# Five groups of small products per mixer unit in place of fourteen

## The chip, the cores and the metric

The kernel runs on one core of a Trainium2 chip. A core has engines that run side by side, each with its own in-order queue: TensorE (PE, with weight loads listed apart as PEld), VectorE (DVE), ScalarE (ACT), GpSimd (POOL) and SyncE (SP, which here only issues DMAs). Products are written by PE into PSUM, which DVE and ACT read. The metric is the device time in microseconds of one execution; the time before is the median of three runs.

## The reference

One layer of a streaming encoder for 1024 frames of a new stream and 32 frames of a running one:

```
h, st = mixer(rms_norm(x, g_mix_pre), ...)      # three head groups, one input and one output projection
x = x + rms_norm(h, g_mix_post)
h, buf = conv_ffn(rms_norm(x, g_ffn_pre), ...)  # up, causal conv, gelu gate, down
x = x + rms_norm(h, g_ffn_post)
```

The mixer has 6 GLA heads (keys of 32), 5 HGRN2 heads and 5 mLSTM heads (keys of 64). GLA and HGRN2 are gated linear scans in chunks of 64 positions:

```
b      = cumsum(log_a)                                     # per chunk and key channel
scores = einsum('bihd,bjhd,bijhd->bijh', q, k, exp(b_i - b_j))   # j <= i
o      = einsum('bijh,bjhv->bihv', scores, v) + einsum('bihk,bhkv->bihv', q * exp(b), s)
s_new  = exp(b_last) * s + einsum('bjhk,bjhv->bhkv', k * exp(b_last - b), v)
```

mLSTM is alike, with one scalar decay per head and a memory `C` with a normaliser column. Head norms and gates follow, then `cat @ w_out`.

## The kernel before, in words

All large products split each fp32 operand into a high and a low part and take three matmuls (`mm3`, lines 101 to 103). Tokens come in three groups: 0 to 383, 384 to 767, and 768 to 1023 with the 32 sample frames. For each group `inproj` (from line 357) computes the input projection on PE: the feature tiles `pf`, convolutions, decays, then the token-major blocks `pv` of values and gates. In the last group `vg_across` computes these blocks feature-major and turns them back with transposes (`back`, line 448): one of the three units behind the first half of the next block, the other two behind its second half, each in a PSUM bank of its own from the pool `psb`, whose tag `big` has three banks.

The recurrent part is the generator `mixer(u, g, ci0)` (line 722), one call per unit of 128 tokens (units 0 to 7) or of the 32 sample frames (unit 8). A unit has two chunks of 64. The exact pairwise decays are built by levels: for c = 32, 16, 8, 4, 2, 1 the positions are split into blocks of 2c, and the second half of a block scores against its first half with decays relative to the block's middle. For one level:

- DVE and ACT make `x` (difference and exponentials), then `Ld` (keys times decay) and `Qz` (queries times decay, lines 847 and 851). `Ld` and `Qz` have two buffers that alternate by level; `x` has three.
- PE makes 16 products of 64 rows and 64 columns into `sc` (one buffer of two banks), 32 matmul records in the profile.
- DVE copies the level's part into the score matrix `P` with a mask (`put`, line 810; the copy is line 815); for c = 32 ACT copies it.

Then come the diagonal `sd`; the state products `up`, in the half banks that `small` hands out in turn (one bank, named `mi` in the profile); the outputs `og` and `oh` (`P` times v, and `qz` times the state `S`); `finish` (norm and gate); the mLSTM scores `sm` with the weights `w`; the transposes of its keys; the memory products `um`; and `oi` and `om`. `sm`, `og`, `oh`, `om`, `oi` share two PSUM banks (tag `o`). Nearly all small products go through the helper `first` (line 718, the matmul itself shows as line 720), which raises their priority by `AHEAD` = 100. [...]

The order of instructions on each engine is made by a scheduler: it simulates the program in time, and takes of the instructions that are ready the one of highest priority, which is by place in the program, with the raised ones ahead. `tc.issue_after(x)` puts what its block issues on x's engine behind x. The mixer yields after each part, and `merge` advances the mixers of the group before by so many steps (`NMIX` = 17 per unit) while a group's `inproj` (`NIN` steps), or the output projection, goes forward. The mixers of the last group (units 8, 6, 7) run beside the output projection of units 0 to 5 and 8; that of 6 and 7 follows. Then comes the feed-forward part (from about 700 us), which the change doesn't touch.

Of the kernel before, what the change touches and what calls it, by code (L numbers as in the profile page):

```python
# [19 lines left out]
DEC = 32  # L20
# [71 lines left out]
def body(ctx: ExitStack, tc: tile.TileContext, a: dict):  # L92
# [264 lines left out]
    def inproj(g, xh, xl, normed, scaled=None):  # L357
# [88 lines left out]
        def vg_across(blks):  # L446

            def back(blk, fs, part):
                for (u, off, n) in units_of(g)[part]:
                    ps = psb.tile([128, 256], F32, tag="big", name=f"pb{u}_{blk}")  # L450
                    for e in range(2):
                        pe.transpose(ps[:n, 128 * e:128 * e + 128], fs[e][:, off:off + n], ident)
                    vg_store(blk, u, off, n, ps)

            before = None
            for blk in blks:
                ws = vg_weights(blk)
                fs = p1.tile([128, 2, T], F32, tag="x", name=f"vf{blk}", bufs=3)
                fs = [fs[:, 0], fs[:, 1]]
                for e in range(2):  # L460
                    ps = psb.tile([128, T], F32, tag="big", name=f"pv{g}_{blk}_{e}")
                    for k in range(8):
                        mm3(ps, [w[:, 128 * e:128 * e + 128] for w in ws[k]], (xh[:, k, :], xl[:, k, :]), k == 0, k == 7)
                    act.copy(fs[e], ps)
# [5 lines left out]
            for e in range(2):  # L470
                back(*before, slice(e, 1 + 2 * e))
# [78 lines left out]
        def rows():  # L550
# [52 lines left out]
            dcs = mx.tile([128, 3, 8], F32, tag="dcs", name=f"dcs{g}", bufs=2)  # L603
            cl = mx.tile([128, 3, 128], F32, tag="cols", name=f"cols{g}", bufs=2)
            if g:
                with tc.high_priority(offset=AHEAD):
                    act.copy(dcs[:, :, :ci], dcp[:, :, :ci])
            for i0, i1 in ((0, 3),) if g == 0 else ((0, 2), (2, 3)):
                if g:
                    yield  # L610
                pt = own[:, :3] if g == 0 else small(i1 - i0, 128)
                for i in range(i0, i1):
                    u, off, n = us[i]
                    pe.transpose(pt[:n, i - i0, :], st[:, off:off + n], ident)
                n = us[i0][2]
                with tc.high_priority(offset=AHEAD):
                    act.copy(cl[:n, i0:i1], pt[:n, :i1 - i0])
                for i in range(i0, i1):
                    cols_of[us[i][0]] = cl[:, i]
            if g == 0:  # L620
# [97 lines left out]
    def first(fn, *args, **kw):  # L718
        with tc.high_priority(offset=AHEAD):
            fn(*args, **kw)  # L720

    def mixer(u, g, ci0):
# [71 lines left out]
        for f0 in (0, 2):  # L794
            kps = small(2, 128)
            for f in (f0, f0 + 1):
                first(pe.transpose, kps[:n, f - f0, :], khf[:, f * n:f * n + n], ident)
            for ch, (o, m) in enumerate(chunks):
                with tc.high_priority(offset=AHEAD):
                    act.copy(kt2[o:o + m, ch, 128 * f0:128 * f0 + 256], kps[o:o + m].rearrange("p f n -> p (f n)"))  # L800
# [23 lines left out]
        li = 0  # L824
        for c in levels:
# [20 lines left out]
            li += 1  # L846
# [7 lines left out]
            sc = psm.tile([128, 1024], F32, tag="sc", name=f"sc{u}_{c}", bufs=1)  # L854
            sc = sc[:, :11 * SCW].rearrange("p (h s) -> p h s", s=SCW)
            for j in range(4):
                for (o, m) in chunks:
                    for hf in range(2):
                        f, q0, q1, p0 = HALVES[hf][j]
                        r = slice(64 * hf, 64 * hf + 64)  # L860
                        mm = c if c == levels[0] else m
                        first(pe.matmul, sc[o:o + mm, p0:p0 + q1 - q0, :m // 2], L[r, f, o:o + mm],
                              Q[r, q0:q1, o // 2:(o + m) // 2], start=True, stop=True)
            if c == levels[0]:
                for (o, m) in chunks:
                    act.copy(P[o:o + c, :, c:2 * c], sc[o:o + c, :, :c])
            else:
                put(c, sc[:n, :, :cl // 2])
            if c == 2:
# [3 lines left out]
                sd = small(11)  # L873
                for f in range(4):
                    first(pe.matmul, sd[:n], z[:, f * n:f * n + n], of_head[:, f, :], start=f == 0, stop=f == 3)
# [6 lines left out]
        Ss = []  # L882
        for ch, (o, m) in enumerate(chunks):
            S = state["S", u == 8]
            Ss.append(S)
            up = small(4, 64)
            for (f, r0, dk, vc) in HEADS:
                first(pe.matmul, up[r0:r0 + dk, f, :], kt2[:n, ch, 128 * f + r0:128 * f + r0 + dk], v[:n, vc:vc + 64],
                          start=True, stop=True)
            Sn = mx.tile([128, 4, 64], F32, tag="S", name=f"S{u}_{ch}", bufs=3)  # L890
            dve.tensor_tensor(Sn, S, dec[:, :, ch:ch + 1].broadcast_to([128, 4, 64]), op=ALU.mult)
            si = dve.tensor_tensor(Sn, Sn, up, op=ALU.add)
            state["S", u == 8] = Sn
        yield

        for (h0, h1, ot) in ((0, 6, og), (6, 11, oh)):
            for h in range(h0, h1):
                f, r0, dk, vc = HEADS[h]
                for ch, (o, m) in enumerate(chunks):
                    first(pe.matmul, ot[o:o + m, OUT[h], :], P[o:o + m, PLANE[h], :m], v[o:o + m, vc:vc + 64],  # L900
                          start=h == h0, stop=False, skip_group_check=True)
        for (h0, h1, ot) in ((0, 6, og), (6, 11, oh)):
            for h in range(h0, h1):
                f, r0, dk, vc = HEADS[h]
                for ch, (o, m) in enumerate(chunks):
                    first(pe.matmul, ot[o:o + m, OUT[h], :], qz[:, h, o:o + m], Ss[ch][:, f, :],
                          start=False, stop=h == h1 - 1, skip_group_check=True)
# [4 lines left out]

        cat = mx.tile([128, 1024], F32, tag="cat", name=f"cat{u}", bufs=1) if u != 7 else ring[0]("cat7")
        ss = mx.tile([128, 16], F32, tag="hss", name=f"hss{u}", bufs=2)
        rs = mx.tile([128, 16], F32, tag="hrs", name=f"hrs{u}", bufs=2)
# [18 lines left out]
        mq, mk = m6[:, 0:3, :], m6[:, 3:6, :]  # L934
        act.copy(mqz[0:64, 0:5:2, :n], mq[0:64, :, :])
        act.copy(mqz[64:128, 1:4:2, :n], mq[64:128, 0:2, :])
        sm = psm.tile([128, 5, 64], F32, tag="o", name=f"sm{u}", bufs=2)
        for f in range(3):
            rows, hs = (128, slice(2 * f, 2 * f + 2)) if f < 2 else (64, slice(4, 5))
            for (o, m) in chunks:  # L940
                first(pe.matmul, sm[o:o + m, hs, :m], mk[:rows, f, o:o + m], mqz[:rows, hs, o:o + m], start=True, stop=True)
        w = mx.tile([128, 320], F32, tag="w", name=f"w{u}", bufs=1)
        w3 = w[:n, :5 * cl].rearrange("p (h n) -> p h n", n=cl)
        dve.tensor_tensor(w3, ab3[:n], cols[:n, 0:5].unsqueeze(2).broadcast_to([n, 5, cl]), op=ALU.add)
        dve.tensor_tensor(w3, w3, caus[:n, :cl].unsqueeze(1).broadcast_to([n, 5, cl]), op=ALU.min)
        act.activation(w3, w3, AF.Exp)
        dve.tensor_tensor(w3, w3, sm[:n, :, :cl], op=ALU.mult)
        yield
        for (h0, h1) in ((0, 4), (4, 5)):
            kp = small(4, 64)  # L950
            if h0 == 0:
                for f in range(2):
                    first(pe.transpose, kp[:n, 2 * f:2 * f + 2, :].rearrange("p h d -> p (h d)"), mk[:, f, :], ident)
            else:
                first(pe.transpose, kp[:n, 0, :], mk[:64, 2, :], ident[:64, :64])
            for ch, (o, m) in enumerate(chunks):
                kwi[0] = dve.tensor_tensor(kw2[o:o + m, ch, h0:h1], kp[o:o + m, :h1 - h0],
                                           cols[o:o + m, 96 + h0:96 + h1].unsqueeze(2).broadcast_to([m, h1 - h0, 64]), op=ALU.mult)
        Cs = []
        for ch, (o, m) in enumerate(chunks):  # L960
            C = state["C", u == 8]
# [956 lines left out]
```

## Time and profile before

| | |
|---|---|
| median of 3 runs | 1377.89 us (1376.87 to 1379.1) |
| profiled execution | 1378.88 us, span of the profile 1377.1 us |
| granted PE clock | 0.989 |
| PE busy | 1326.5 us (96%) |
| DVE busy | 1029.4 us (75%) |
| ACT busy | 705.0 us (51%) |
| POOL busy | 313.1 us (23%) |
| mean DMA rate | 196 GB/s |

An engine's busy time is the time in which at least one of its instructions runs. Matmuls overlap in a pipeline, so what one costs is read from the distance between starts, not from its own duration. A row of the timeline has the start and length in us, engine, line, operation, the output and inputs by name, the weights' rows*columns, the form and a count; idle time before it stands in brackets with what ended it. The mixers' products lie between about 150 and 650 us.

### The profile page before, as it was taken

Reading aid. Unit: us, or ns where it says so; the run is one execution under the profiler, and the core shown is the slowest. Engines: PE = TensorE matmul, PEld = TensorE weight load, DVE = VectorE, ACT = ScalarE, POOL = GpSimd, SP = SyncE. Lnnn points to the kernel's source line nnn. Section 1 sums busy time; section 2 is a strip of 40 time slices with the busy share of each in tenths; the row PEclk is TensorE's granted clock in tenths of the full one; section 3 lists DMA queues with packets and bytes.
Section 4 is the critical chain, followed back from the end, with each engine's and each line's share of the span. In section 5 each row is a group of like instructions: output and inputs, shape, how many; then the busy total and the mean of one; then the engine's idle time right before and its main releaser. Section 6 shows DMA issues by size and latency. Waiting matters only on the chain.

```text
span 1377.1 us, 29219 instructions
## 1 busy us (share of the span) xinstructions
PE 1326.5 (96%) x11472; PEld 1198.8 (87%) x11472; DVE 1029.4 (75%) x1916; ACT 705.0 (51%) x1369; POOL 313.1 (23%) x529
## 2 busy tenths in 40 slices
PE   6999999999999898999989999999999999999997
PEld 5999889898889786867879999999999997678885
DVE  4786458768587669685989888888888876399566
ACT  4555447445475547342665555555455545454552
POOL 5532411226012154222211112111121110010005
PEclk9999999999999999999999999999999999999998
DMA  9699778876789936543423565655374239744435
GB/s 342 203 318 363 262 243 284 260 262 207 262 261 316 336 96 198 176 130 88 168 66 116 163 177 136 150 141 156 107 184 129 87 113 394 274 152 133 147 110 123
DMA packets 125825, 269.72 MB, mean 196 GB/s; under 512 B 24007, under 2 KB 59367, under 8 KB 125607
## 3 DMA queue, kind: packets, MB, share of 16 engines
q1 hardware_dynamic: 111959, 245.43, 52.9%
q0 software_dynamic: 8928, 18.09, 7.1%
q10 hardware_dynamic: 4800, 4.33, 0.9%
q8 instruction: 90, 1.47, 0.4%
q14 instruction: 48, 0.39, 0.1%
HBM read 206.72 MB, written 86.18 MB: 213 GB/s over the span
## 4 chain that ended last, share of the span: by engine, by line
PE 75%; DVE 10%; DMA 6%; ACT 5%; issue 2%; POOL 1%; SPq 1%; DVEq 0%; ACTq 0%; POOLq 0%
PE pux L101 4%; PE pux L102 4%; PE pux L103 4%; PE pv L101 4%; PE pv L103 4%; PE pv L102 4%; PE puw L102 3%; PE puw L103 3%; PE puw L101 3%; PE q L101 3%; PE q L102 3%; PE q L103 3%; PE x L101 2%; PE x L102 2%; PE x L103 2%; PE zp L101 2%
## 5 line engine op out<-in xcount | busy, mean ns | idle before, releaser
L1341 DVE SCALAR_TENSOR_TENSOR y<-uu,fconv_sb,y 128x1060 f32<-128x1060 f32 x88 | 116.2, 1321 | 36.7 <-ACT y L1339 35.8
L1277 ACT COPY c<-pux 128x272 f32<-128x272 f32 (+1 forms) x132 | 49.3, 376 | 50.1 <-PE pux L103 46.5
L101 PE MATMUL pv<-wt_0h,xh 128*128 128x256 f32 (+2 forms) x195 | 57.7, 296 | 5.4 <-ACT xh L321 4.8
L1339 ACT ACTIVATE y<-uu,fconv_sb 128x1060 f32<-128x1060 f32 x44 | 56.1, 1274 | 12.1 <-POOL uu L1335 10.8
L101 PE MATMUL zp<-woh,ch 128*128 128x512 f32 (+1 forms) x144 | 59.4, 414 | 2.4 <-DVE z L1156 1.2
L1338 POOL COPY fhalo<-uu 128x2 f32<-128x2 f32 x44 | 17.1, 388 | 184.2 <-DVE uu L1282 184.2
L102 PE MATMUL zp<-wol,ch 128*128 128x512 f32 (+1 forms) x144 | 57.9, 402 | 0.0
L103 PE MATMUL zp<-woh,cl 128*128 128x512 f32 (+1 forms) x144 | 57.8, 402 | 0.0
L103 PE MATMUL pv<-wt_1h,xl 128*128 128x256 f32 (+2 forms) x195 | 57.1, 293 | 0.0
L103 PE MATMUL pv<-wt_0h,xl 128*128 128x256 f32 (+2 forms) x195 | 56.7, 291 | 0.4 <-DVE xl L322 0.4
L101 PE MATMUL pv<-wt_1h,xh 128*128 128x256 f32 (+2 forms) x195 | 56.9, 292 | 0.0
L102 PE MATMUL pv<-wt_1l,xh 128*128 128x256 f32 (+2 forms) x195 | 56.8, 291 | 0.0
L102 PE MATMUL pv<-wt_0l,xh 128*128 128x256 f32 (+2 forms) x195 | 56.2, 288 | 0.1
L1517 POOL TENSOR_TENSOR gss<-gss 128x1 f32<-128x1 f32 (+1 forms) x9 | 8.1, 899 | 186.8 <-ACT gjk L1510 186.8
L220 POOL TENSOR_SCALAR hrs<-hss 128x5 f32<-128x5 f32 (+3 forms) x27 | 9.6, 356 | 161.2 <-DVE hss L922 159.8
L101 PEld LDWEIGHTS pv<-wt_0h,xh 128*128 128x128 f32 (+1 forms) x195 | 36.8, 189 | 7.4 <-ACT xh L321 5.7
L431 POOL TENSOR_TENSOR vg<-vth,gh 128x256 f32<-128x256 f32 (+1 forms) x36 | 29.2, 812 | 61.6 <-DMA vm<-v_d 22.0
L815 DVE COPY_PREDICATED P<-masks_sb,sc 128x352 f32<-128x352 int32 (+1 forms) x44 | 29.8, 677 | 11.8 <-PE sc L720 11.5
L851 DVE TENSOR_TENSOR Qz<-x,qe 128x128 f32<-128x128 f32 (+1 forms) x106 | 29.8, 298 | 11.7 <-PE sc L720 11.0
L103 PEld LDWEIGHTS pv<-wt_0h,xl 128*128 128x128 f32 (+1 forms) x195 | 37.1, 190 | 1.2 <-DVE xl L322 0.9
L101 PEld LDWEIGHTS pv<-wt_1h,xh 128*128 128x128 f32 (+1 forms) x195 | 37.6, 193 | 0.4 <-issue 0.2
L103 PEld LDWEIGHTS pv<-wt_1h,xl 128*128 128x128 f32 (+1 forms) x195 | 37.4, 192 | 0.6 <-issue 0.2
(1718 smaller groups left out, 5384.3 us busy)
## 6 DMA issues: line engine op xcount, KB each, us to landing
wrP<-in_w_dn SPq DMA_DIRECT2D x27, 512.0 KB, 3.4
h_d<-y SPq DMA_DIRECT2D x22, 530.0 KB, 2.8
ht<-h_d SPq DMA_DIRECT2D x22, 530.0 KB, 8.8
wt_0r<-in_w_tok SPq DMA_DIRECT2D x21, 512.0 KB, 5.2
wt_1r<-in_w_tok SPq DMA_DIRECT2D x21, 512.0 KB, 6.8
ws_d<-in_w_dn POOLq DMA_DIRECT2D x20, 512.0 KB, 8.7
wrP<-ws_d SPq DMA_DIRECT2D x20, 512.0 KB, 4.2
wt_0l<-lt_d SPq DMA_DIRECT2D x14, 512.0 KB, 4.1
```

What stands on the lines that cost most here:

```text
L101: pe.matmul(ps, lh[0], rh[0], start=first, stop=False, **kw)
L102: pe.matmul(ps, lh[0], rh[1], start=False, stop=False, **kw)
L103: return pe.matmul(ps, lh[1], rh[0], start=False, stop=last, **kw)
L220: pool.tensor_scalar(out, ss, 1.0 / width, eps, op0=ALU.mult, op1=ALU.add)
L431: pool.tensor_tensor(o[:n], th[:n], gh[:n, c0:c0 + 256], op=ALU.mult)
L815: dve.copy_predicated(dst, mk.broadcast_to([n, 11, *mk.shape[2:]]), src)
L851: dve.tensor_tensor(Qp[:, 2 * i, :, :n // 2].rearrange("p e (m c) -> p e m c", c=c), second(x4[:, f:f + 1], c).broadcast_to([128, 2, n // ...
L1277: kept[name] = act.copy(t, ps)
L1338: behind["POOL"] = pool.tensor_copy(fhalo[:, j, :], u[:, NCOL - 2:NCOL])
L1339: act.activation(y, u, AF.Identity, scale=fconv[:, j, 2:3], bias=fconv[:, j, 3:4])
L1341: dve.scalar_tensor_tensor(y, uu[i][:, s:s + NCOL], fconv[:, j, s:s + 1], y, op0=ALU.mult, op1=ALU.add)
L1517: pool.tensor_tensor(ss[:n, 0:1], ss[:n, 2:3], ss[:n, 3:4], op=ALU.add)
```

## The change

A unit's small products are collected into five groups:

1. the scores of the levels 32 and 16, then the transposes of the keys `khf`;
2. the scores of 8 and 4, then the mLSTM scores `sm` and the transposes of its keys;
3. the scores of 2 and 1, then the diagonal `sd` (now in the free columns of the `sc` tile) and the state products of both chunks;
4. the outputs `og` and `oh`, then the memory products `um` of both chunks;
5. `oi` (last chunk first) and `om`.

Two levels share one `sc` tile, side by side. In each group the product whose operands are computed last is issued first (`lead`), and the rest is put behind it with `issue_after`. The level's products start with the features whose `Qz` is written last. DVE and ACT work is the same but is written at other places: the `mqz` copies and the weights `w` come ahead of the second group instead of behind `finish`. The priority of the small products is 400 (`SOON`) instead of 100. Unit 8 has the levels 16 to 1, so its last group of scores has one level.

Beside this, `back` makes the transposes of all three units at once behind the second half of a block, two units in one bank and the third in another; the row statistics of groups 1 and 2 are transposed in one tile of their own in `psb` instead of in half banks of `small`; and `NMIX` is 11, since a unit has 9 steps instead of 15.

```diff
-            def back(blk, fs, part):
-                for (u, off, n) in units_of(g)[part]:
-                    ps = psb.tile([128, 256], F32, tag="big", name=f"pb{u}_{blk}")
+            def back(blk, fs):
+                us = units_of(g)
+                whole = psb.tile([128, 2, 256], F32, tag="big", name=f"pb{us[0][0]}_{blk}")
+                rest = psb.tile([128, 256], F32, tag="big", name=f"pb8_{blk}")
+                pss = [whole[:, 0], whole[:, 1], rest]
+                for (u, off, n), ps in zip(us, pss):
                     for e in range(2):
                         pe.transpose(ps[:n, 128 * e:128 * e + 128], fs[e][:, off:off + n], ident)
+                for (u, off, n), ps in zip(us, pss):
                     vg_store(blk, u, off, n, ps)
...
-                    if before:
-                        back(*before, slice(e, 1 + 2 * e))
+                    if before and e:
+                        back(*before)
...
-            own = psm.tile([128, 4, 128], F32, tag="o", name="rows0", bufs=2) if g == 0 else None
-            dcp = small(3, 8) if g else own[:, 3, :24].rearrange("p (a b) -> p a b", b=8)
+            own = (psb if g else psm).tile([128, 4, 128], F32, tag="big" if g else "o", name=f"rows{g}", bufs=3 if g else 2)
+            dcp = own[:, 3, :24].rearrange("p (a b) -> p a b", b=8)
...
-    def first(fn, *args, **kw):
-        with tc.high_priority(offset=AHEAD):
+    SOON = 400
+
+    def soon(fn, *args, **kw):
+        with tc.high_priority(offset=SOON):
             fn(*args, **kw)
...
+        def scores(sc, c, L, Q, at, lead=None):
+            ins = None
+            with tc.issue_after(lead.ins) if lead else ExitStack():
+                for j in (3, 0, 1, 2):
+                    for (o, m) in chunks:
+                        for hf in range(2):
+                            f, q0, q1, p0 = HALVES[hf][j]
+                            r = slice(64 * hf, 64 * hf + 64)
+                            mm = c if c == levels[0] else m
+                            with tc.high_priority(offset=SOON):
+                                x = pe.matmul(sc[o:o + mm, p0:p0 + q1 - q0, at:at + m // 2], L[r, f, o:o + mm],
+                                              Q[r, q0:q1, o // 2:(o + m) // 2], start=True, stop=True)
+                            ins = ins or x
+            return ins
...
+        for l0 in range(0, len(levels), 2):
+            pair = [operands(c, i) for i, c in enumerate(levels[l0:l0 + 2])]
+            last_pair = pair[-1][0] == levels[-1]
...
+            lead = scores(sc, *pair[-1], (len(pair) - 1) * (cl // 2))
+            if len(pair) == 2:
+                scores(sc, *pair[0], 0, lead)
+            sd = sct[:, 11 * SCW:11 * SCW + 11]
+            with tc.issue_after(lead.ins):
+                if l0 == 0:
+                    keys()
+                elif l0 == 2:
+                    memory_scores()
+                if last_pair:
+                    for f in range(4):
+                        soon(pe.matmul, sd[:n], z[:, f * n:f * n + n], of_head[:, f, :], start=f == 0, stop=f == 3)
+                    si = states()
...
+        lead = None
         for (h0, h1, ot) in ((0, 6, og), (6, 11, oh)):
             for h in range(h0, h1):
                 f, r0, dk, vc = HEADS[h]
                 for ch, (o, m) in enumerate(chunks):
...
+        with tc.issue_after(lead.ins):
+            for (h0, h1, ot) in ((0, 6, og), (6, 11, oh)):
...
+            memories()
...
+        lead = None
+        for ch, (o, m) in reversed(list(enumerate(chunks))):
+            for h in range(5):
+                with tc.high_priority(offset=SOON), tc.issue_after(lead.ins) if lead else ExitStack():
+                    x = pe.matmul(oi[o:o + m, h, :], mqz[:, h, o:o + m], Cs[ch][:, h // 2, :], start=True, stop=True)
+                lead = lead or x
+        with tc.issue_after(lead.ins):
+            for h in range(5):
+                for ch, (o, m) in enumerate(chunks):
+                    soon(pe.matmul, om[o:o + m, h, :], w[o:o + m, h * cl:h * cl + m], vmt[o:o + m, h, :], start=True, stop=True)
...
-    NMIX, NIN = 17, 12 + 2 + 24
+    NMIX, NIN = 11, 12 + 2 + 24
```

The functions `keys`, `memory_scores`, `states` and `memories` hold the products and copies that the loop body had before, in the same form: first the products of both chunks, then the additions on DVE that read them.

More of the change, by code (lines that the diff above doesn't have):

```diff
@@ L469, in vg_across @@
                 yield
-            for e in range(2):
-                back(*before, slice(e, 1 + 2 * e))
+            back(*before)
         tgs = pf.tile([128, 3, 26], F32, tag="tgs", name=f"tgs{g}")
@@ L822, in mixer, with operands @@
                     act.activation(qe[:, i, e, :n], q4[:, f, :], AF.Copy, scale=parity[:, i, e:e + 1])
-        li = 0
-        for c in levels:
+        def operands(c, li):
             x = mx.tile([128, 512], F32, tag="x", name=f"x{u}_{c}", bufs=NX)
@@ L864, in mixer @@
[L864 to L869, printed above, removed]
+            return c, L, Q
+        def scores(sc, c, L, Q, at, lead=None):
[12 more added lines that the diff above has]
+            return ins
@@ new lines, in mixer, with keys @@
+        mq, mk = m6[:, 0:3, :], m6[:, 3:6, :]
+        cat = mx.tile([128, 1024], F32, tag="cat", name=f"cat{u}", bufs=1) if u != 7 else ring[0]("cat7")
+        ss = mx.tile([128, 16], F32, tag="hss", name=f"hss{u}", bufs=2)
+        rs = mx.tile([128, 16], F32, tag="hrs", name=f"hrs{u}", bufs=2)
+        def keys():
+            for f0 in (0, 2):
+                kps = small(2, 128)
+                for f in (f0, f0 + 1):
+                    soon(pe.transpose, kps[:n, f - f0, :], khf[:, f * n:f * n + n], ident)
+                for ch, (o, m) in enumerate(chunks):
+                    with tc.high_priority(offset=AHEAD):
+                        act.copy(kt2[o:o + m, ch, 128 * f0:128 * f0 + 256], kps[o:o + m].rearrange("p f n -> p (f n)"))
@@ L932, in mixer @@
         yield
[L934 to L958, printed above, removed]
```

173 lines of the change are left out of this document (90 added, 83 removed).

## The prediction

> **What bounds the kernel now.** I read the page's busy times first, then the windows that cut the span into stages, then TensorE's (PE's) timeline in the stage that the change touches, then what PE and VectorE (DVE) wait for there.
>
> ```profile
> PE 1326.5 (96%) x11472; PEld 1198.8 (87%) x11472; DVE 1029.4 (75%) x1916; ACT 705.0 (51%) x1369; POOL 313.1 (23%) x529
> ```
> ```profile
> PE 75%; DVE 10%; DMA 6%; ACT 5%; issue 2%; POOL 1%; SPq 1%; DVEq 0%; ACTq 0%; POOLq 0%
> ```
> ```profile
> 150.00:226.00 76.00, 73.99 (x758) 65.80 (x757) 47.52 (x111) 42.79 (x82) 10.80 (x15) 0.98 0.75 244
> 226.00:345.00 119.00, 116.87 (x1523) 108.53 (x1522) 90.99 (x211) 62.99 (x132) 41.01 (x59) 1.00 0.77 255
> 345.00:510.00 165.00, 159.46 (x2012) 143.76 (x2011) 114.99 (x308) 88.29 (x209) 38.72 (x62) 0.98 0.78 261
> 510.00:660.00 150.00, 142.77 (x1457) 109.70 (x1457) 115.71 (x243) 66.08 (x147) 45.20 (x70) 0.98 0.48 148
> ```
> ```profile
> 400.00:450.00 50.00, 47.16 (x608) 43.25 (x604) 41.49 (x108) 30.10 (x70) 9.51 (x20) 0.97 0.94 307
> 510.00:560.00 50.00, 45.26 (x412) 35.47 (x411) 45.08 (x100) 29.34 (x62) 21.53 (x27) 0.97 0.51 163
> ```
>
> The columns behind the length are busy microseconds of PE, weight loads, DVE, ScalarE (ACT) and GpSimd, then PE's clock, the DMA share and GB/s. The mixers lie in 150 to 660 us. PE is busy 493.1 of those 510 us, so 16.9 us are idle, and over the whole span 75% of the chain that ended last (the row that begins with PE 75%) is PE's. Two stretches are different: at 400 to 450 the DMA engines are at 0.94, and at 510 to 560 DVE is busy 45.08 us of 50, as much as PE. What is saved on PE there is not all saved in time. Behind 700 us nothing changes.
>
> How much of PE's time is the mixers' small products? The same windows restricted to their one helper line (720) end in this row:
>
> ```profile
> sum 510.00, PE 141.14 PEld 112.42; mean PE 35.28 PEld 28.11
> ```
>
> That is 141 of 510 us. The small products do not stand in one block per unit. On the timeline PE leaves the large 128*128 matmuls, does some products with 64- or 32-wide tiles, and returns. I call that a visit. There are 99 visits of the mixers, of which these are the beginning of the first and the end of the last:
>
> ```profile
> 153.64 0.55 PE L720 MATMUL sc<-Qz,Ld 64*32 64x64 f32 x32
> ...
> 647.90 0.80 PE L720 MATMUL om<-vm,w 64*64 64x65 f32 x20
> ```
>
> **What a visit costs.** Columns: start, us, line, tile, rows*columns, count.
>
> ```profile
> 238.14 0.34 PE L102 MATMUL pf<-xl,wf_12h 128*128 128x384 f32 x1
> 238.41 0.69 PE L720 MATMUL sc<-Qz,Ld 64*64 64x64 f32 x32
> 239.02 0.45 PE L103 MATMUL pf<-xh,wf_12l 128*128 128x384 f32 x1
> 239.31 0.34 PE L101 MATMUL pf<-xh,wf_12h 128*128 128x384 f32 x1
> 239.49 0.34 PE L102 MATMUL pf<-xl,wf_12h 128*128 128x384 f32 x1
> ...
> 241.95 0.34 PE L101 MATMUL pf<-xh,wf_12h 128*128 128x384 f32 x1
> 242.12 0.38 PE L720 MATMUL mi<-ident,kh 128*128 128x128 f32 x2
> 242.26 0.42 PE L102 MATMUL pf<-xl,wf_12h 128*128 128x384 f32 x1
> 242.52 0.34 PE L103 MATMUL pf<-xh,wf_12l 128*128 128x384 f32 x1
> ...
> 243.23 0.34 PE L101 MATMUL pf<-xh,wf_13h 128*128 128x384 f32 x1
> 243.50 0.55 PE L720 MATMUL sc<-Qz,Ld 64*64 64x64 f32 x24
> 243.98 0.44 PE L720 MATMUL mi<-ident,kh 128*128 128x128 f32 x2
> 244.35 0.34 PE L720 MATMUL sc<-Qz,Ld 64*64 64x64 f32 x8
> 244.62 0.44 PE L102 MATMUL pf<-xl,wf_13h 128*128 128x384 f32 x1
> 244.90 0.34 PE L103 MATMUL pf<-xh,wf_13l 128*128 128x384 f32 x1
> ```
> ```profile
> 277.84 0.28 PE L102 MATMUL pv<-wt_0l,xh 128*128 128x256 f32 x1
> 278.05 0.27 PE L720 MATMUL mi<-ident,mqk 64*128 64x64 f32 x1
> 278.25 0.39 PE L103 MATMUL pv<-wt_0h,xl 128*128 128x256 f32 x1
> 278.47 0.28 PE L101 MATMUL pv<-wt_0h,xh 128*128 128x256 f32 x1
> ```
>
> Large matmuls of 384 columns follow each other every 0.18 us (239.31 to 239.49). From 238.14 to 239.31 there are two such steps, 0.35 us, and one score level, so the visit costs 1.17 - 0.35 = 0.82 us. Its 32 records take at most the 0.61 us between their first start and the next large one, so at least 0.21 us of the visit is fixed. A visit of one record (0.63 us less two steps of 0.12) costs 0.39 us, nearly all of it fixed. So a visit's fixed price lies between 0.21 and 0.39 us; I take the middle, 0.30.
>
> Two full-size (128*128) transposes alone cost 0.57 - 0.35 = 0.22 us. Put between the scores they make the visit 1.67 - 0.35 = 1.32 us, against 0.82 + 0.22 apart: 0.28 us for two changes of tile shape inside a visit, 0.14 each. So shape decides, not the number of products.
>
> [...]
>
> **The change part by part.** The profiled execution took 1378.88 us, 1.0 above the median of 1377.89; the sum is made against it.
>
> 1. *Groups.* A unit's six score levels come as three pairs; the key transposes go behind the first pair, the memory scores and their transposes behind the second, the diagonal and the state products behind the third; the memory products go behind the outputs; and both mLSTM outputs together. That is five groups. I add one visit per unit, since the last 64*128 key transpose needs the half bank that VectorE is still reading, so PE will do something large in between. Nine units make 54 visits instead of 99: 45 x 0.30 = 13.5 us less (45 x 0.21 = 9.5 to 45 x 0.39 = 17.6). No product is added or removed.
>
> 2. *Changes of shape inside a visit.* Counted along the timeline there are 130 besides entering and leaving. After it I count from the code about ten per full unit (one in the first group, two or three in the second, five in the third, one in each of the last two), some 90. 40 x 0.14 = 5.6 us at best, 0 if the scheduler mixes them; I take 3.
>
> 3. *What isn't on the path.* The two stretches above are 100 of 510 us, so I strike a fifth of 16.5: 3.3 us.
>
> 4. *Waiting at the head.* The rest of a group is queued behind the product whose operand comes last. All large matmuls behind it in PE's queue wait too. PE's largest wait today before small products, from the rows of line 720 (us, times):
>
> ```profile
>   DVE Qz L851: 4.8, 7
> ```
>
> That is 0.7 us each. With fewer heads and one wait per group there are fewer chances to wait; but a group that the schedule places too early waits for more. I take 3 us off the 16.9 idle (8 less to 8 more).
>
> 5. *Double buffers.* `Ld` and `Qz` have two buffers, which used to serve successive levels. A pair takes both, so VectorE can't write the next pair's operands until the scores of this one are done. Mean ns of each:
>
> ```profile
> L815 DVE COPY_PREDICATED P<-masks_sb,sc 128x352 f32<-128x352 int32 x40 | 28.0, 701 | 11.4 <-PE sc L720 11.3
> L851 DVE TENSOR_TENSOR Qz<-x,qe 128x128 f32<-128x128 f32 x92 | 27.1, 311 | 11.1 <-PE sc L720 11.0
> L841 DVE TENSOR_TENSOR Ld<-x,qkb 128x256 f32<-128x256 f32 x38 | 17.1, 450 | 3.4 <-ACT x L838 3.4
> L847 DVE TENSOR_TENSOR Qz<-x,qkb 128x128 f32<-128x128 f32 x46 | 15.0, 326 | 5.8 <-PE sc L720 5.8
> ```
>
> One level's operands are 0.45 + 0.33 + 2 x 0.31 = 1.40 us behind the release. That lengthens a unit's chain by up to 3 x 1.4 = 4.2 us, but three round trips of PE and VectorE go as well, each with a `P` copy of 0.70 and a wait for `sc`. And the memory part no longer follows the outputs. I cost it at nothing: DVE is idle 140.8 of the 510 us, and PE has large matmuls to do meanwhile. Without that cover it is the slower rival.
>
> 6. *Banks.* The gate transposes of a block now hold two of the three `big` banks at once, so the next block's product waits for the copy of the one before:
>
> ```profile
> PE pv L101 <- ACT vf L464: 0.8, 1, 0.8
> ```
>
> Once 0.8 us today; at most seven blocks, 5.6 us; PE does the transposes meanwhile, so I take 1. The row tiles of groups 1 and 2 also move to a `big` bank, for two copies each; hidden by the other two banks.
>
> 7. *Order.* A mixer now has 9 steps instead of 15, spread over the same main work, and its products get priority 400 instead of 100. No DMA is added, but the mixers' loads on SP's queue stand between other weight loads than before:
>
> ```profile
> wt_0r<-in_w_tok SPq DMA_DIRECT2D x21, 512.0 KB, 5.2
> ```
>
> One load later or earlier where PE waits for it is 5.2 us either way; I take 0. The mLSTM weights and `mqz` copies are the same instructions earlier; ACT, half idle, takes them.
>
> Sum: -13.5 - 3 + 3.3 - 3 + 1 = -15.2 us: 1378.9 - 15.2 = 1363.7, so 1364.
>
> **The rivals.**
>
> *The groups come apart or the gain is hidden.* The scheduler orders by its own idea of when operands are ready, and 45 becomes 20 visits fewer: 20 x 0.30 = 6, less a fifth, 4.8, less the bank's 1 is 3.8: 1375. For it: today fourteen steps already appear as eleven visits, so the schedule isn't the program. Against: the explicit queueing behind the lead.
>
> *Slower: the pair's shared buffers.* The place is 510 to 660 us, where units 8, 6 and 7 must pass before the last output projection. If their chain sets the end, three units x 4.2 = 12.6 us come on top and PE's gain is idle time: 1378.9 + 12.6 = 1391. It decides once the three units grow by more than the 7.2 us that PE is idle there, 2.4 per unit. For it: DVE's 45.08 of 50, and the 11.1 + 5.8 us that the `Qz` writes already wait for scores. Against: PE is busy 142.77 of those 150 us today, and the round trips halve.
>
> *The change doesn't do what it says: no fixed price.* If small products cost by the record only, nothing goes: 1378.9 less or plus the banks, 1379. The 0.39 us of one record speaks against it. [...]
>
> **How the numbers follow.** Forecast 0.66, groups apart 0.10, slower 0.16, no fixed price 0.08. The forecast's own range is 1350 (17.6 + 6 + 8, less a fifth of 23.6, is 27 off, and the bank's 0) to 1374 (9.5 less a fifth is 7.6, the bank 3). About 0.2%, 2.8 us, is what a measurement can tell here. Faster: 0.66 and most of the 1375 case, 0.74; same: the rest and most of the last, 0.07; slower 0.19. For 8 in 10 the range goes up into the slower case, to 1386, and down to 1349.
>
> **What would show it.** Right: about 55 visits instead of 99 in 150 to 660 us, 64 score records in a row, PE's idle there no more than 17 us, and the large matmuls of the output projection ending some 15 us earlier. Step 1 is wrong if score visits of 32 are still frequent; step 4 if PE's waits for `Qz` grow past 15 us; step 5 if VectorE's waits for `sc` grow and PE idles at 510 to 660; step 6 if `pv` waits for `vf` in each block. Wrong altogether if the small products cost as much in fewer visits.

## The result, and the profile after

The changed kernel takes 1549.12 us (1541.85 to 1552.47), the kernel before 1379.4 us beside it: 1.122 of before, with an interval from 1.120 to 1.124. The forecast was 1364, and even the slower rival ended at 1391.

TensorE's busy time, the chain that ended last by engine and by line, and three of the groups that grew, from the page after; then two of these groups in the kernel before, and the clock of after and of before:

```profile
PE 1484.3 (96%) x11472; PEld 1312.0 (85%) x11472; DVE 1029.6 (67%) x1916; ACT 707.5 (46%) x1368; POOL 322.1 (21%) x529
...
PE 80%; DVE 9%; DMA 5%; ACT 3%; issue 2%; POOL 1%; SPq 0%; DVEq 0%; ACTq 0%; POOLq 0%
PE sc L854 6%; PE mi L717 6%; PE pux L103 4%; PE pux L102 4%; PE pux L101 4%; PE pv L101 3%; PE pv L103 3%; PE pv L102 3%; PE puw L102 3%; PE puw L101 3%; PE puw L103 3%; PE pf L101 2%; PE pf L103 2%; PE pf L102 2%; PE q L101 2%; PE q L103 2%
...
L910 DVE TENSOR_TENSOR S<-S,mi 128x256 f32<-128x256 f32 x17 | 7.1, 419 | 108.5 <-PE mi L717 108.2
L854 PE MATMUL sc<-Qz,Ld 64*64 64x32 f32 (+5 forms) x1344 | 74.4, 239 | 0.0
...
L717 PE MATMUL mi<-v,kt 128*32 128x64 f32 (+3 forms) x374 | 68.5, 280 | 0.0
```
```profile
L720 PE MATMUL sc<-Qz,Ld 64*64 64x32 f32 (+5 forms) x1344 | 34.0, 220 | 1.9 <-DVE Qz L851 1.9
L720 PE MATMUL mi<-v,kt 128*32 128x64 f32 (+3 forms) x374 | 15.7, 229 | 0.5 <-DVE P L815 0.4
```
```profile
core 0: 1540.1 us, clock 0.945
```
```profile
core 0: 1377.1 us, clock 0.989
```

The number of TensorE's products is that of before, 11472, and it is busy 157.8 us more. It hardly waits more: idle time is 1540.1 - 1484.3 = 55.8 us against 50.6. The others wait for it: VectorE stands 108.2 us in front of the state update until the state products are done. So the same products take longer. The timeline of the third group of one unit shows how (start, length, line, product, tile, form, count):

```profile
325.28 0.29 PE L103 MATMUL pv<-wt_1h,xl 128*128 128x256 f32 x1
325.49 0.33 PE L854 MATMUL sc<-Qz,qkb 64*64 64x64 f32 x2
325.75 0.39 PE L101 MATMUL pv<-wt_0h,xh 128*128 128x256 f32 x1
326.06 0.30 PE L854 MATMUL sc<-Qz,qkb 64*64 64x32 f32 x2
326.29 0.30 PE L717 MATMUL mi<-v,kt 128*32 128x64 f32 x2
326.52 0.33 PE L854 MATMUL sc<-Qz,qkb 64*64 64x64 f32 x2
326.78 0.30 PE L717 MATMUL mi<-v,kt 128*32 128x64 f32 x2
...
329.66 0.33 PE L717 MATMUL mi<-v,kt 128*64 128x64 f32 x2
329.92 0.42 PE L854 MATMUL sc<-Qz,qkb 64*64 64x32 f32 x2
330.27 0.47 PE L717 MATMUL mi<-v,kt 128*64 128x64 f32 x2
330.67 0.42 PE L854 MATMUL sc<-Qz,qkb 64*64 64x32 f32 x2
...
340.41 0.85 PE L854 MATMUL sc<-Qz,Ld 64*64 64x64 f32 x18
341.19 1.88 PE L717 MATMUL sc<-cf_sb,x 128*128 128x11 f32 x8
342.91 0.56 PE L102 MATMUL pv<-wt_0l,xh 128*128 128x256 f32 x1
...
346.69 0.40 PE L101 MATMUL pv<-wt_1h,xh 128*128 128x256 f32 x1
346.90 0.30 PE L102 MATMUL pv<-wt_1l,xh 128*128 128x256 f32 x1
347.04 0.28 PE L103 MATMUL pv<-wt_1h,xl 128*128 128x256 f32 x1
```

The lead went alone (325.49), a full-size (128*128) product slipped in behind it, and then the scores and the state products, which `issue_after` had made ready together, take turns by two records. From 326.06 to 329.66 there are 15 steps in 3.60 us, 0.24 each. From 329.92 on a step takes 0.35 to 0.41, and the 256-column products behind the group follow each other by 0.21 us instead of 0.12 until 346.90. The windows of 3 us (busy time of PE, weight loads, VectorE, ScalarE, GpSimd, then the clock, DMA share, GB/s) name the reason:

```profile
327.00:330.00 3.00, 3.00 (x27) 2.14 (x26) 0.00 (x0) 0.00 (x0) 0.00 (x0) 0.98 0.98 324
330.00:333.00 3.00, 3.00 (x17) 2.22 (x18) 0.00 (x0) 0.00 (x0) 0.00 (x0) 0.50 0.81 326
...
342.00:345.00 3.00, 3.00 (x16) 3.00 (x16) 1.86 (x2) 0.00 (x0) 0.00 (x0) 0.50 0.00 0
345.00:348.00 3.00, 3.00 (x20) 3.00 (x20) 0.98 (x2) 0.30 (x1) 0.00 (x0) 0.68 0.03 5
348.00:351.00 3.00, 3.00 (x27) 2.33 (x25) 0.00 (x0) 0.08 (x1) 0.00 (x0) 1.00 0.13 44
```

After about four microseconds of alternation (326.06 to 329.92) the granted clock is half (0.98 up to 330, then 0.50), though the profile shows PE busy without a gap, and it comes back 4.0 us after the large products have (342.91 to 346.90). The same happens in the third group of each of the eight full units: the clock records have half clock for 13.7 or 17.1 us there, and for 3.4 and 6.8 us in the fourth group of two units, each time after four microseconds in which PE is busy without a gap and the shape changes 12 to 16 times. These ten stretches are 130 us; the kernel before has none that begins like this.

Counted along the timeline of the mixers' stage from 150 us on, with sides rounded up to 32, 64 or 128 for the count, the changes of tile shape rose from 376 to 855, while the runs of small tiles between full-size products fell from 107 to 77. (The prediction counted the mixers' own products alone, so it has 99 visits for the 107 here.)

### The profile page after: what moved, and what is told of

Its sections match the earlier page's. It is cut to its first block, busy times and chain, and to the rows that moved or that the text cites. A ratio compares the mean times of both kernels' runs of the same rounds, so it can differ in the third digit from the quotient of the medians.

```text
span 1540.1 us, 29153 instructions
## 1 busy us (share of the span) xinstructions
PE 1484.3 (96%) x11472; PEld 1312.0 (85%) x11472; DVE 1029.6 (67%) x1916; ACT 707.5 (46%) x1368; POOL 322.1 (21%) x529
## 4 chain that ended last, share of the span: by engine, by line
PE 80%; DVE 9%; DMA 5%; ACT 3%; issue 2%; POOL 1%; SPq 0%; DVEq 0%; ACTq 0%; POOLq 0%
PE sc L854 6%; PE mi L717 6%; PE pux L103 4%; PE pux L102 4%; PE pux L101 4%; PE pv L101 3%; PE pv L103 3%; PE pv L102 3%; PE puw L102 3%; PE puw L101 3%; PE puw L103 3%; PE pf L101 2%; PE pf L103 2%; PE pf L102 2%; PE q L101 2%; PE q L103 2%
## 5 line engine op out<-in xcount | busy, mean ns | idle before, releaser
L910 DVE TENSOR_TENSOR S<-S,mi 128x256 f32<-128x256 f32 x17 | 7.1, 419 | 108.5 <-PE mi L717 108.2
L854 PE MATMUL sc<-Qz,Ld 64*64 64x32 f32 (+5 forms) x1344 | 74.4, 239 | 0.0
L854 PEld LDWEIGHTS sc<-Qz,Ld 64*64 64x64 f32 (+2 forms) x1344 | 52.1, 144 | 22.1 <-issue 10.0
L717 PE MATMUL mi<-v,kt 128*32 128x64 f32 (+3 forms) x374 | 68.5, 280 | 0.0
L1379 POOL COPY fhalo<-uu 128x2 f32<-128x2 f32 x44 | 16.5, 374 | 177.8 <-DVE uu L1323 177.7
L805 DVE COPY_PREDICATED P<-masks_sb,sc 128x352 f32<-128x352 int32 (+3 forms) x53 | 37.9, 715 | 13.1 <-PE sc L717 12.3
L717 PEld LDWEIGHTS mi<-v,kt 128*32 128x32 f32 (+3 forms) x374 | 35.6, 144 | 12.7
```

What stands on the lines that cost most here:

```text
L805: dve.copy_predicated(dst, mk.broadcast_to([n, 11, *mk.shape[2:]]), src)
L854: x = pe.matmul(sc[o:o + mm, p0:p0 + q1 - q0, at:at + m // 2], L[r, f, o:o + mm], Q[r, q0:q1, o // 2:(o + m) // 2], start=True, stop=True)
L1379: behind["POOL"] = pool.tensor_copy(fhalo[:, j, :], u[:, NCOL - 2:NCOL])
```

## The experiments

The theory was: the alternation costs the time, by a price per change of shape and through the clock. The rivals: the raised priority, the block products (`back`), the pairs' shared buffers. All of these kernels compute the whole result, and each ratio is to runs of the kernel before on the same chip, whose medians were 1377.7 to 1380.9 us.

**Is it the alternation?** First each tail is queued behind the last product of the stream before it instead of behind the lead:

```diff
...
                             ins = ins or x
+            tip[0] = x
             return ins
...
-            with tc.issue_after(lead.ins):
+            with tc.issue_after(tip[0].ins):
                 if l0 == 0:
                     keys()
...
-                        soon(pe.matmul, ot[o:o + m, OUT[h], :], qz[:, h, o:o + m], Ss[ch][:, f, :],
-                              start=False, stop=h == h1 - 1, skip_group_check=True)
-            memories()
+                        with tc.high_priority(offset=SOON):
+                            x = pe.matmul(ot[o:o + m, OUT[h], :], qz[:, h, o:o + m], Ss[ch][:, f, :],
+                                          start=False, stop=h == h1 - 1, skip_group_check=True)
+        with tc.issue_after(x.ins):
+            memories()
```


> The changed kernel, with the tail of each group (key transposes, memory scores, diagonal, state products, memory products) queued behind the group's last score or last output product in place of its first one. In PE's program order the changes of tile shape fall from 895 to 322 (342 before). Theory A (PE alternates between the streams of a group, and pays a change of shape each time): about 1375 us, 1365 to 1390, and the clock back to 0.985 or more. Theory B (a pair of levels takes both Ld and Qz buffers): nothing of that is mended, 1530 or more. Theory C (priority 400 displaces the large products): not mended either, 1530 or more.

Measured: 1402.01 us, 1.0157 [1.0129, 1.0185]; clock 0.979, 357 changes. Of the 169.7 us, 148.6 are gone; the time is still 12 us above the range expected for the alternation alone, and the clock below the 0.985. A group's scores are one row again:

```profile
332.35 1.14 PE L856 MATMUL sc<-Qz,Ld 64*64 64x64 f32 x64
333.42 0.44 PE L717 MATMUL mi<-ident,kh 128*128 128x128 f32 x2
```

The same for the diagonal and the states of the third group alone:

```diff
...
                 elif l0 == 2:
                     memory_scores()
+            with tc.issue_after(tip[0].ins):
                 if last_pair:
```


> The changed kernel, with only the diagonal and the state products of the third group queued behind its last score; the other groups as changed. 572 changes of shape in PE's order. Theory A: 553 more changes cost 170 us, 0.31 us each with what the slower clock adds; 230 more than before are 71 us: 1450 us, 1425 to 1475. Theories B and C: 1530 or more.

Measured: 1437.38 us, 1.0415 [1.0389, 1.0440], 553 changes, within the range expected for the alternation. The third group alone holds 112 us, two thirds of the loss. And the changed kernel with the old priority:

```diff
-    SOON = 400
+    SOON = 100
```


> The changed kernel with priority 100 in place of 400, nothing else; the groups' streams still alternate, 932 changes of shape against 895. If alternation and priority add: 1549 - 23 + 37 x 0.27 = 1536 us, 1515 to 1555. If priority is what makes the streams alternate: below 1450.

Measured: 1547.43 us, 1.123 [1.1197, 1.1264], 909 changes. The priority doesn't make the alternation.

**Two other parts of the change, each alone in the kernel before.** Priority 400 for `first`:

```diff
+    SOON = 400
...
     def first(fn, *args, **kw):
-        with tc.high_priority(offset=AHEAD):
+        with tc.high_priority(offset=SOON):
```


> The kernel before with the small products' priority at 400 in place of 100, nothing else. 351 changes of shape, 342 before. Theory A: within 5 us of 1379. Theory C: a large part of the 170 us, 1450 or more. Theory B: no change.

Measured: 1403.62 us, 1.017 [1.014, 1.020], with 374 changes against 376. None of the three expectations fits: it costs 22.7 us without more changes. Here PE does stand still; scores were put into its queue long before their buffer was free:

```profile
465.71 0.29 PE L103 MATMUL pv<-xh,wt_0l 128*128 128x288 f32 x1
473.13 0.85 PE L721 MATMUL sc<-Qz,Ld 64*64 64x64 f32 x20 [7.12 <-ACT P L867]
```

And the new `back`, with all three units behind the second half of a block:

```diff
...
-                    if before:
-                        back(*before, slice(e, 1 + 2 * e))
+                    if before and e:
+                        back(*before)
...
```


> The kernel before with only the changed turning back of the gate blocks (three units at once, two banks held). 349 changes of shape, 342 before. The prediction's step 6 gives 1 us more, 0 to 5.6: 1380 us, within 6 of before.

Measured: 1390.41 us, 1.0084 [1.0060, 1.0108]. It costs 12.7 us, but not by the wait that the prediction named: `pv` waiting for `vf` isn't among this run's waits in 150 to 670 us at all.

**Are fewer visits worth anything once the order is kept?** The first edit plus chains inside the tails: key transposes behind the memory scores, states behind the scores, diagonal behind the states.

```diff
...
+                        tip[0] = pe.matmul(sm[o:o + m, hs, :m], mk[:rows, f, o:o + m], mqz[:rows, hs, o:o + m], start=True, stop=True)
+            behind = ExitStack()
+            behind.enter_context(tc.issue_after(tip[0].ins))
             for (h0, h1) in ((0, 4), (4, 5)):
...
+            behind.close()
...
+                if last_pair:
+                    si = states()
+            if last_pair:
+                with tc.issue_after(tip[0].ins):
+                    for f in range(4):
+                        soon(pe.matmul, sd[:n], z[:, f * n:f * n + n], of_head[:, f, :], start=f == 0, stop=f == 3)
-                    si = states()
```

(`tip[0]` is then the last memory score or, set inside `states`, the last state product.)

> As e1, and inside the tails too each kind of product is queued behind the last of the kind before: memory scores, then their key transposes; scores, state products, then the diagonal. 228 changes of shape, 114 fewer than before the change. Theory A with the price of the prediction (0.14 to 0.19 us per change): 16 to 22 us less than before, 1360 us (1352 to 1370). Theory B: 1530 or more, or at least the 1391 of the slower rival if only the last stage suffers.

Measured: 1398.65 us, 1.0138 [1.0107, 1.0170]: not the 1360 that fewer changes alone would give. Then the same with the lower priority:

```diff
-    SOON = 400
+    SOON = 100
```


> As e4, with the small products' priority back at 100. 257 changes of shape in PE's order. If the 23 us that priority 400 cost the kernel before (e3) are the rest of the loss in e4: 1399 - 23 = 1376 us, 1366 to 1384. If what keeps e4 above 1380 is the pair's shared buffers, as the slower rival has it, the priority changes little: 1390 or more.

Measured: 1391.77 us, 1.0098 [1.0061, 1.0134]; the intervals overlap, and the priority isn't the rest of the loss. And with the block products of before as well:

```diff
...
-                    if before and e:
-                        back(*before)
+                    if before:
+                        back(*before, slice(e, 1 + 2 * e))
...
```


> As e5, with the turning back of the gate blocks as before. 259 changes of shape. By the prediction's step 6 within 6 us of e5 and not slower; 1375 us if e5 is 1376.

Measured: 1389.88 us, 1.0081 [1.0051, 1.0110]; not told apart from the run without that edit. Its timeline has the groups as the change meant them:

```profile
472.71 1.14 PE L853 MATMUL sc<-Qz,Ld 64*64 64x64 f32 x64
473.77 0.92 PE L882 MATMUL sm<-mqz,mqk 128*64 128x128 f32 x12
...
479.76 1.78 PE L908 MATMUL mi<-v,kt 128*32 128x64 f32 x44
481.47 1.06 PE L714 MATMUL sc<-cf_sb,x 128*128 128x11 f32 x8
482.38 0.38 PE L101 MATMUL pv<-xh,wt_0h 128*128 128x288 f32 x1
```

From start to start the 64 scores take 1.06 us and the 44 state products 1.71, so two records in order take 0.033 and 0.078, on average 0.055, against 0.24 in turns (at a clock of 0.98 to 1.00): from these rows I estimate 0.185 us for a change of shape at full clock. (These rows hold a few changes themselves, so it is if anything more. The expectations of the later runs take 0.17 for it.) This kernel has 295 changes instead of 376 and still loses 12 us. A place where it loses (the timeline, then windows of 2 us):

```profile
341.53 0.66 PE L318 MATMUL xt<-ident,x 128*128 128x128 f32 x4 [0.19 <-ACT vth L113]
345.07 0.60 PE L101 MATMUL pv<-wt_0h,xh 128*128 128x282 f32 x1 [2.88 <-DVE xl L322]
345.47 0.44 PE L102 MATMUL pv<-wt_0l,xh 128*128 128x282 f32 x1
```
```profile
340.00:342.00 2.00, 1.81 (x31) 1.31 (x30) 2.00 (x6) 2.00 (x5) 1.76 (x3) 1.00 0.94 217
342.00:344.00 2.00, 0.19 (x2) 0.00 (x0) 1.25 (x4) 1.95 (x6) 1.97 (x3) 1.00 0.79 287
344.00:346.00 2.00, 0.93 (x4) 0.93 (x5) 2.00 (x5) 1.46 (x4) 1.49 (x3) 0.53 0.99 389
...
352.00:354.00 2.00, 2.00 (x11) 1.99 (x10) 0.00 (x0) 0.50 (x3) 0.00 (x0) 0.50 0.00 0
354.00:356.00 2.00, 2.00 (x54) 1.61 (x52) 1.46 (x4) 1.10 (x3) 0.00 (x0) 0.91 0.20 66
```

PE waits 2.88 us for VectorE, and then runs some nine microseconds at half clock (0.50 in the windows from 346 to 354): the wait of 2.88 us and between four and five more are lost here.

**Which part keeps the chained kernel behind?** Here `NMIX` follows the number of steps (12 to 14). First the key transposes ahead of the levels again:

```diff
+        keys()
+        yield
         for l0 in range(0, len(levels), 2):
...
-                if l0 == 0:
-                    keys()
```


> The chained kernel with the block products of before (1389.9 us against 1377.7 for the kernel before, some 12 us slower although TensorE's order holds 259 changes of tile shape instead of 342), with one part more undone: the transposes of the decayed keys are issued ahead of the levels again, as in the kernel before, not behind the first group's last score. Order now 262 changes. If the 12 us are TensorE standing at those transposes (in the run without this edit the waits ended by ACT's copy of kt come to 7.1 us in 150 to 670 us): 7 us less, about 1.003 of before. If only changes of shape cost: no difference, 1.008 to 1.010. If the two levels of a group hold each other up through their shared operand buffers: no difference, 1.008 to 1.010.

Measured: 1388.15 us, 1.0066 [1.0049, 1.0084]. That is 2 us of the 12, and the intervals overlap; the 7 us expected, if PE stood at these transposes, are not there. The gate columns in small banks as before, in addition:

```diff
...
-            own = (psb if g else psm).tile([128, 4, 128], F32, tag="big" if g else "o", name=f"rows{g}", bufs=3 if g else 2)
-            dcp = own[:, 3, :24].rearrange("p (a b) -> p a b", b=8)
+            own = psm.tile([128, 4, 128], F32, tag="o", name="rows0", bufs=2) if g == 0 else None
+            dcp = small(3, 8) if g else own[:, 3, :24].rearrange("p (a b) -> p a b", b=8)
...
```


> As the run before it in this list, and the gate columns go back to the small banks in pieces as in the kernel before (order 248 changes). If the 12 us come from the gate columns' tile, which takes a bank of the large products: 3 to 6 us under the run without this edit. If not: the same as that run within 2 us, since 14 changes at 0.17 us are 2.4 us.

Measured: 1393.44 us, 1.0107 [1.0093, 1.0121]; not the cause: 5 us slower, where at most 6 faster was expected. In addition each level alone:

```diff
-        for l0 in range(0, len(levels), 2):
-            pair = [operands(c, i) for i, c in enumerate(levels[l0:l0 + 2])]
+        for l0 in range(0, len(levels)):
+            pair = [operands(c, l0) for c in levels[l0:l0 + 1]]
```


> As the run before it in this list, and each level is a group of its own again with the operand buffers in turn, as in the kernel before; the queueing of the kinds behind one another stays (order 289 changes, against 342 of the kernel before). If the pairs' shared operand buffers are what is lost: under the kernel before, by up to 53 changes x 0.17 = 9 us, ratio 0.993 to 0.998. If changes of shape alone count: 41 changes x 0.17 = 7 us over the run with pairs. If the loss is in what is left (the memory scores taken ahead of the outputs, old-memory products ahead of om, 14 steps of the order for 17): still 1.004 to 1.010.

Measured: 1394.24 us, 1.0112 [1.0098, 1.0126]. And these two lines alone in the chained kernel with the old `back`:

> The chained kernel with the block products of before, and only the pairs undone: levels one by one, key transposes behind the first level's scores and gate columns in one tile as in the changed kernel (order 287 changes). If the pairs' shared buffers are the loss: 1.000 or below. If the key transposes' place or the gate columns are: as the chained kernel, 1.008, or 28 changes x 0.17 = 5 us more, 1.011.

Measured: 1398.12 us, 1.0146 [1.0129, 1.0162], 8 us slower than with pairs. Undoing the pairs gains nothing, so the rival, with 12.6 us for the shared buffers, falls. It also adds 24 and 25 changes, by the price above 4 to 5 us, so a smaller cost of the buffers isn't excluded. The last runs ask whether the small products are still raised too far: priority 30, and 0, on the kernel with the key transposes ahead, and 30 on the kernel before.

```diff
-    SOON = 100
+    SOON = 30
```


> The kernel with the chained groups and the key transposes ahead of the levels, with priority 30 for the small products instead of 100 (order 265 changes of shape against 262). It stands 10 us above the kernel before although it has 76 changes fewer on the timeline; by the account of changes, idle time and clock it loses 10.9 us in idle time and 13.9 in clock. If that is TensorE's queue standing at small products placed ahead of their operands because they are raised too far: idle 5 to 10 us less and with it most of the clock, 1370 to 1380. If the chaining itself makes it stand: no difference, 1385 to 1392.

Measured: 1390.29 us, 1.0058 [1.0036, 1.0081]. And with `SOON = 0`:

> As the run before it in this list, with no raised priority at all (order 250 changes). By the theory of priority: as low as that run or lower, 1365 to 1380, unless the mixers now come late and the last units end behind the output projection, then over 1395. By the theory of the chaining itself: 1385 to 1392.

Measured: 1395.06 us, 1.0100 [1.0085, 1.0115]. And the kernel before, where `first` takes 30 for `AHEAD`:

> The kernel before with priority 30 for its small products instead of 100 (order 352 changes against 342). Priority 400 cost it 23 us, by idle time (10) and clock (14). If a lower priority takes idle time away in the same way: 1370 to 1377, less 10 changes x 0.17 = 2 us. If 100 is low enough that the products wait for nothing more: 1377 to 1381.

Measured: 1395.4 us, 1.0104 [1.0082, 1.0126]. A lower priority gives nothing back either, and costs the kernel before 14 us, which no expectation had.

**An account of all runs.** Three numbers of each profile, against the kernel before: changes of shape on the timeline at 0.185 us; idle time (span less PE's busy time); and clock (one less the mean clock, times the span). Since span less idle time is busy time, what this tests is whether the growth of PE's busy time beyond the slower clock follows the changes at one price.

| kernel | changes | at 0.185 | idle | clock | sum | span of the profile |
|---|---|---|---|---|---|---|
| after | 855 | +88.6 | +5.2 | +69.6 | +163 | +163.0 |
| tails queued in order | 357 | -3.5 | +13.7 | +14.2 | +24 | +22.6 |
| states' tail alone | 553 | +32.7 | +3.9 | +20.8 | +57 | +59.8 |
| after, priority 100 | 909 | +98.6 | +2.2 | +73.0 | +174 | +168.5 |
| before, priority 400 | 374 | -0.4 | +10.3 | +14.2 | +24 | +20.7 |
| before, new `back` | 384 | +1.5 | +6.3 | +5.7 | +13 | +12.3 |
| chained | 268 | -20.0 | +24.5 | +19.7 | +24 | +18.8 |
| chained, priority 100 | 293 | -15.4 | +13.8 | +9.8 | +8 | +8.1 |
| the same, old `back` | 295 | -15.0 | +16.1 | +9.9 | +11 | +12.9 |
| keys ahead | 300 | -14.1 | +10.9 | +13.9 | +11 | +8.5 |
| keys ahead, old columns | 293 | -15.4 | +17.0 | +14.1 | +16 | +15.3 |
| the same, single levels | 318 | -10.7 | +13.7 | +15.5 | +18 | +16.5 |
| chained, single levels | 319 | -10.5 | +11.2 | +19.7 | +20 | +17.2 |
| keys ahead, priority 30 | 302 | -13.7 | +12.5 | +15.5 | +14 | +14.3 |
| keys ahead, priority 0 | 287 | -16.5 | +14.7 | +19.7 | +18 | +15.5 |
| before, priority 30 | 386 | +1.9 | +9.2 | +4.4 | +15 | +14.0 |

Sum and span agree within 5.4 us in every row. By this account the saving that the prediction counted on is there in the chained kernels, 10 to 20 us, and it is spent on idle time (+10.9 to +24.5) and on the clock (+9.8 to +19.7). No order that was run has as little of both as the kernel before, and no version beat it. Which of the waits is to blame in the chained kernels stays open: they lie in other places in each run, before `oi`, `og`, `pv` and the key transposes, and no single undone part removed them.

## Why the prediction was wrong

*Step 1, groups.* Right in kind, too large in number: 45 visits fewer were forecast, and it is 30 (107 to 77; in the chained kernel with the old `back` 19, to 88, about what the rival of groups coming apart had). A visit has two changes of shape more than none, 0.37 us by the price measured here, inside the 0.21 to 0.39 and above the 0.30 taken.

*Step 2, changes inside a visit: this is the step that failed.* It counted changes from the order of the code, 130 down to 90, and bounded the other end with "0 if the scheduler mixes them". The count less two for each visit went from 162 to 701. The price (0.14, measured 0.185) was of the right size, a quarter low; the 540 changes more come to some 100 us at full clock, less 11 for the 30 visits. Zero wasn't the bound: products made ready together may be taken in turns, and the worst case was every pair of records a change. The queueing behind the lead, which the prediction held against the groups coming apart, is what made both streams ready at once.

*The clock had no step.* It is 69.6 of the 163 us. The prediction read 0.98 and 1.00 in its window rows as given and asked nothing of what the change does to it.

*Step 3, off the path.* Nothing of the loss was hidden; PE's share of the chain rose from 75 to 80%. What part of a saving would be hidden no run shows, since none was faster.

*Step 4, waiting at the head.* -3 (-8 to +8); measured +5.2 in the changed kernel over the whole span, inside the bounds. That is luck: with the alternation undone it is +11 to +25, outside.

*Step 5, double buffers.* Costed at nothing, and no run speaks against it beyond the 4 to 5 us above; pairs undone gave +0.8 and +8 us.

*Step 6, banks.* 1 (0 to 5.6); alone it costs 12.7, and not by the wait for `vf`; in the chained kernel the same edit makes no difference that can be told. By the account it is idle time and clock; which wait brings it stays open.

*Step 7, order.* 0; priority 400 alone costs the kernel before 22.7 us, by the account idle time (+10.3) and clock (+14.2); PE stands in its queue at products that can't start yet, like the one of 7.12 us. In the changed kernel it makes no difference.

*The range.* Its fast end adds up to 1352, not 1350, and its slow end leaves out the 8 us of step 4. Neither matters beside 1549.

*The rivals.* The slower one had the right direction by luck: its place and mechanism were wrong. "No fixed price" falls: the same products took another time in another order, two score records 0.033 us in an unbroken row (64 records in 1.06 us) and a step of two records 0.24 us in turns. What the time did follow, beside idle time and clock, is the changes of tile shape at the 0.185 us estimated above for each: with them sum and span agree within 5.4 us in every row.

## What to carry to other kernels

Grouping small products cost 12.2% here while the kinds were dealt out in turns, and still 0.6% at best with each kind in one piece: queue a stream behind the last product of the one before it, not behind its first, and count the changes of tile shape in the order that the engine really gets, since what is ready together may be dealt out in turns, here by two records at 0.24 us a step. Read the granted clock beside the busy time, in windows of a few microseconds: from 330 to 333 us of the changed kernel TensorE was busy all 3.00 us at a clock of 0.50. Count with a wait in TensorE's queue what comes behind it: the one of 2.88 us was followed by slow time that cost between four and five more.

## What the runs showed of the hardware

In the changed kernel the granted clock fell to 0.50 after some four microseconds of alternating tile shapes (12 to 16 changes in each of ten places; 326.06 to 329.92 in the one shown), while the profile had TensorE busy without a gap; it came back 4.0 us after large products resumed (342.91 to 346.90). In the profiles of before and after the stretches of half clock that end before the kernel does last 3.41 to 17.07 us; the shortest, 3.41 us, takes up to 1.7 us of TensorE's time. By what the alternation brings the clock down no run shows, and the little work of the small products isn't ruled out as a part of it; shown is that with the alternation undone the mean clock rises from 0.945 to 0.979. Half clock was also seen behind waits: the gap of 2.88 us was followed by 0.50, and in the kernel before a wait of 1.85 us (for ScalarE's copy of `kt`, to 412.39 us) was followed by a clock of 0.50 from 414 to 417 us.
